# Splitting float32 weights by two GpSimd-issued DMAs and one ACT negation, in place of an ACT cast and a GpSimd subtraction

## The chip, the cores and the metric

One core of one Trainium2 chip runs the whole program in one launch. The metric is the device time of that launch in microseconds. The kernel before takes 3497.29 us (median of 3 runs, 3495.54 to 3500.16).

## The reference, cut to what matters

The model has ten parts in a row, each of them working on the same residual of 512 tokens by 1024 features in float32: twice a mixer (attention beside a gated delta net, m0 and m1) and a feed-forward layer (f0, f1), then an even mixer (ev), cross-attention with a memory (xa0), a feed-forward layer (g0), an odd mixer (od), cross-attention (xa1) and a feed-forward layer (g1). Nearly all of the arithmetic is products of activations with weights, as in the feed-forward layers of the first block:

```python
h = rmsnorm(x, norm_ffn_g[l])
u = centred_depthwise_conv(h @ w_up[l], ffn_conv_w[l])      # 1024 -> 2 * 2816
u_gate, u_val = jnp.split(u, 2, axis=-1)
x = x + ((jax.nn.silu(u_gate) * u_val) @ w_down[l])         # 2816 -> 1024
```

The products must have float32 accuracy. The kernel gets it from three products of a faster format, float32r: with w = hi + lo and a = hi' + lo', it sums hi·hi', hi·lo' and lo·hi'.

## The kernel before, in words

Activations are held feature-major, as eight chunks of 128 features by 512 tokens, each as its two float32r parts (`act`, or `mid` behind the gate of a feed-forward layer). A **group** of weights is 128 output columns times eight chunks of 128 input rows. Its product (`proj`, lines 480 to 491) is 24 matmuls into one PSUM bank: for each chunk hi with the first part of the activation (L487), hi with the second (L490), lo with the first (L491).

The weights come through `wload` (L464). One DMA on SP's queue (`fetch`, L461) brings 256 columns, 1 MB, into `wraw`, which has two buffers. Each half group, 128 columns by four chunks, is then split: ACT rounds it to float32r (`whi`, L474), GpSimd subtracts that from the raw weights (`wlo`, L475, which is recorded as L383). `whi` and `wlo` have four buffers of half a group each, so two groups are split ahead, and `wraw` holds up to four groups more.

A feed-forward layer works in 11 **pairs** (`up_pair`): it loads two groups of the gate (A and B) and two of the value (C and D), and TensorE needs them in the order A, C and B mixed, D. The results go through DVE, ACT and (in g0 and g1, `up2`) one GpSimd product `cv<-cv,rB` into `mid`. After five, nine and eleven pairs `down` adds to the residual (`out_proj`).

The instructions are put into order, engine by engine, by a scheduler that models time while the program is built; each engine then works in that order and waits for semaphores. SP's queue carries, besides the weights, all scratch transfers of the mixers.

Of the kernel before, what the change touches and what calls it, by code (L numbers as in the profile page):

```python
# [11 lines left out]
F32 = mybir.dt.float32  # L12
F32R = mybir.dt.float32r
# [48 lines left out]
def _vec_layout(inputs=None):  # L62
    """All per-feature vectors as columns of one [128, n] array; fills VEC with the places."""
# [19 lines left out]
        # (dir, pair) columns, the head of the pair by partition half  # L83
# [26 lines left out]
def _const_layout():  # L110
    """Constants of the shapes alone, [128, n] float32."""
# [94 lines left out]
def host_arrays(inputs):  # L206
# [15 lines left out]
    # z, and the rows of its product's projection: heads 0 2, 1 3, 4 6, 5 7 side by side  # L222
# [4 lines left out]
    A["win"] = _pack_cols(np.concatenate([kd, qd, vd, qa, ka, va, z, gate], axis=-1), 8, 256)  # L227
# [3 lines left out]
    A["wout"] = _pack_cols(g("w_out"), 8, 256)  # L231
    A["wup"] = _pack_cols(g("w_up"), 8, 256)
    for nm, key in (("wdn", "w_down"), ("fdn", "ffn_w_out_2")):
        w = g(key)
        A[nm] = np.concatenate([_pack_cols(w[:, :1024], 8, 256), _pack_cols(w[:, 1024:2048], 8, 256)], axis=1)
        A[nm + "c"] = _pack_cols(w[:, 2048:], 6, 256)
# [3 lines left out]
    A["evin"] = _pack_cols(np.concatenate(ev, axis=2).reshape(1, D, 4096), 8, 256)  # L240
    A["evout"] = _pack_cols(np.concatenate([eo[:, 1 - i, h] for i, h in EV_HEADS], axis=1), 8, 256)
    # by head: q, k, v columns side by side
    od = g("od_w_in_2").reshape(1, D, 3, 8, P).transpose(0, 1, 3, 2, 4).reshape(1, D, 3072)
    A["odin"] = _pack_cols(od, 8, 256)
    A["odout"] = _pack_cols(g("od_w_out_2"), 8, 256)
    A["xaq"] = _pack_cols(g("xa_w_q_2"), 8, 256)
    A["xakv"] = _pack_cols(g("xa_w_kv_2"), 8, 256)
    A["xao"] = _pack_cols(g("xa_w_o_2"), 8, 256)
    A["fup"] = _pack_cols(g("ffn_w_in_2"), 8, 256)
# [10 lines left out]
# ---------------------------------------------------------------- the program  # L260
class Norm:
    """RMS norm of the feature-major residual: chunks x*g split in two float32r parts; the
    reciprocal root of each token, on all partitions, is applied where products leave PSUM."""
# [8 lines left out]
    def chunk(self, m):  # L272
# [12 lines left out]
        # the sums of the last chunk apart, the others' are done by then  # L285
# [20 lines left out]
class Prog:  # L306
    def __init__(self, ctx, tc, A, out, first):
# [5 lines left out]
        self.wr = pool("wr", 2)  # L313
# [13 lines left out]
        # the first weights amid the residual  # L327
        self.first = []
        for m in range(8):
            nc.sync.dma_start(out=self.x[m], in_=A["x"][m])  # L330
            if m == 1:
                self.first = [self.fetch(s, 8, n) for s, n in first]
# [7 lines left out]
    def banks(self, *bufs):  # L340
        """The PSUM banks besides those of the projections, in up to three rings."""
# [11 lines left out]
    def phase(self, name):  # L353
        """The pool of a layer part: temporaries by role."""
# [3 lines left out]
    def gs(self, name, bufs=2, shape=(P, S), dt=F32):  # L358
        """A temporary of a role: its buffers go round in program order."""
# [40 lines left out]
    def issue_behind(self, ins, before):  # L400
        """Issue order on an engine, no wait."""
# [56 lines left out]
    # ---- weights  # L458
    def fetch(self, src, kc, cg):
        raw = self.wr.tile([P, kc, cg], F32, name="wraw", tag="wraw")  # L460
        self.nc.sync.dma_start(out=raw, in_=src.rearrange("p (k c) -> p k c", k=kc))  # L461
        return raw
# [1319 lines left out]
```

## Time and profile before

| | |
|---|---|
| time, median of 3 runs | 3497.29 us |
| span of the profiled execution | 3496.1 us |
| TensorE busy | 3232.1 us, 92% |
| VectorE (DVE) busy | 2028.2 us, 58% |
| ScalarE (ACT) busy | 1483.6 us, 42% |
| GpSimd (POOL) busy | 1806.7 us, 52% |
| DMA moved | 342.51 MB, mean 98 GB/s |

The profile gives no time of its own for the profiled execution beside its span of 3496.1 us, first to last instruction; that is 1.2 us under the median of the runs. PE is TensorE's matmuls and PEld its weight loads, which lie beside each other. A busy time says how long an engine had work in hand; a wait is the idle time before an instruction, put down to what ended it. Matmuls overlap in the pipeline, so the distance between their starts, not their duration, is what one costs.

The ten parts can be told apart by the copy `rB` (L303) that ends each norm. By it m0 runs from 0 to 552 us, f0 to 917, m1 to 1437, f1 to 1803, ev to about 2080, xa0 to 2302, g0 to 2669, od to about 2920, xa1 to 3141 and g1 to 3496.

### The profile page before, as it was taken

Reading aid. Unit: us, or ns where it says so; the run is one execution under the profiler, and the core shown is the slowest. Engines: PE = TensorE matmul, PEld = TensorE weight load, DVE = VectorE, ACT = ScalarE, POOL = GpSimd, SP = SyncE. Lnnn points to the kernel's source line nnn. Section 1 sums busy time; section 2 is a strip of 40 time slices with the busy share of each in tenths; the row PEclk is TensorE's granted clock in tenths of the full one; section 3 lists DMA queues with packets and bytes.
Section 4 is the critical chain, followed back from the end, with each engine's and each line's share of the span. In section 5 each row is a group of like instructions: output and inputs, shape, how many; then the busy total and the mean of one; then the engine's idle time right before and its main releaser. Section 6 shows DMA issues by size and latency. Waiting matters only on the chain. (4 is left out here: it accounts for less than half of the span.)

```text
span 3496.1 us, 46894 instructions
## 1 busy us (share of the span) xinstructions
PE 3232.1 (92%) x17342; PEld 2661.3 (76%) x17342; DVE 2028.2 (58%) x3571; ACT 1483.6 (42%) x2766; POOL 1806.7 (52%) x1493
## 2 busy tenths in 40 slices
PE   8878899999978889999999888999997799899999
PEld 6666778888766677888878777888885687878887
DVE  8988556463698855555466676552323586663222
ACT  4536434343553553434353335443433355544332
POOL 4653365444565335554456556465554235556554
PEclk9999999999999999999999999999998899999999
DMA  4532532222353244222222113222223312222222
GB/s 142 161 88 61 132 122 86 100 94 94 122 159 102 72 113 128 87 97 97 94 101 86 59 62 109 73 97 97 97 91 91 84 61 103 91 90 89 95 98 93
DMA packets 135844, 342.51 MB, mean 98 GB/s; under 512 B 43039, under 2 KB 80287, under 8 KB 106944
## 3 DMA queue, kind: packets, MB, share of 16 engines
q1 hardware_dynamic: 135328, 338.75, 30.5%
q8 instruction: 138, 2.26, 0.3%
q14 instruction: 90, 0.74, 0.1%
q10 hardware_dynamic: 288, 0.76, 0.1%
HBM read 309.53 MB, written 29.95 MB: 97 GB/s over the span
## 5 line engine op out<-in xcount | busy, mean ns | idle before, releaser
L383 POOL TENSOR_TENSOR wlo<-wraw,whi 128x512 fp32r<-128x512 f32 (+2 forms) x1044 | 1370.2, 1316 | 1449.5 <-ACT whi L474 1402.0
L474 ACT CAST whi<-wraw 128x512 fp32r<-128x512 f32 (+2 forms) x1044 | 631.4, 608 | 1134.3 <-PE psb L490 838.4
L487 PE MATMUL psb<-act,whi 128*128 128x512 f32 x1888 | 760.6, 403 | 60.3 <-DVE x L383 19.8
L491 PE MATMUL psb<-act,wlo 128*128 128x512 f32 x1888 | 752.7, 399 | 3.5 <-POOL wlo L383 3.4
L490 PE MATMUL psb<-act,whi 128*128 128x512 f32 x1888 | 755.0, 400 | 0.6 <-DVE act L277 0.6
L487 PEld LDWEIGHTS psb<-act,whi 128*128 128x128 f32 x1888 | 364.5, 193 | 140.8 <-issue 43.0
L491 PEld LDWEIGHTS psb<-act,wlo 128*128 128x128 f32 x1888 | 363.4, 192 | 81.6 <-POOL wlo L383 5.8
L490 PEld LDWEIGHTS psb<-act,whi 128*128 128x128 f32 x1888 | 364.3, 193 | 74.2 <-DVE act L277 1.9
L383 DVE TENSOR_TENSOR x<-psb,x 128x512 f32<-128x512 f32 x168 | 115.2, 689 | 378.1 <-PE psb L491 377.5
L487 PE MATMUL ps<-act,whi 128*128 128x512 f32 (+1 forms) x720 | 281.6, 391 | 3.4 <-ACT rB L303 3.4
L491 PE MATMUL ps<-act,wlo 128*128 128x512 f32 (+1 forms) x720 | 281.0, 390 | 0.0
L490 PE MATMUL ps<-act,whi 128*128 128x512 f32 (+1 forms) x720 | 281.0, 390 | 0.0
L487 PE MATMUL psb<-mid,whi 128*128 128x512 f32 x704 | 277.0, 394 | 1.0 <-DVE x L383 1.0
L491 PE MATMUL psb<-mid,wlo 128*128 128x512 f32 x704 | 276.2, 392 | 0.0
L490 PE MATMUL psb<-mid,whi 128*128 128x512 f32 x704 | 274.1, 389 | 0.0
L487 PEld LDWEIGHTS ps<-act,whi 128*128 128x128 f32 (+1 forms) x720 | 134.1, 186 | 33.8 <-ACT rB L303 4.6
L491 PEld LDWEIGHTS ps<-act,wlo 128*128 128x128 f32 (+1 forms) x720 | 134.1, 186 | 29.8 <-issue 0.8
L490 PEld LDWEIGHTS ps<-act,whi 128*128 128x128 f32 (+1 forms) x720 | 134.2, 186 | 29.3 <-issue 0.5
L491 PEld LDWEIGHTS psb<-mid,wlo 128*128 128x128 f32 x704 | 132.3, 188 | 30.3
L487 PEld LDWEIGHTS psb<-mid,whi 128*128 128x128 f32 x704 | 132.6, 188 | 29.4 <-DVE x L383 1.5
L490 PEld LDWEIGHTS psb<-mid,whi 128*128 128x128 f32 x704 | 132.3, 188 | 29.1
L383 DVE TENSOR_TENSOR cv<-ps,cv 128x512 f32<-128x512 f32 (+1 forms) x60 | 41.5, 692 | 175.8 <-PE ps L491 106.1
(437 smaller groups left out, 5712.8 us busy)
## 6 DMA issues: line engine op xcount, KB each, us to landing
wraw<-in_wup SPq DMA_DIRECT2D x44, 1024.0 KB, 4.8
wraw<-in_fup SPq DMA_DIRECT2D x44, 1024.0 KB, 4.8
wraw<-in_win SPq DMA_DIRECT2D x38, 1024.0 KB, 5.0
wraw<-in_wdn SPq DMA_DIRECT2D x16, 1024.0 KB, 4.8
wraw<-in_evin SPq DMA_DIRECT2D x16, 1024.0 KB, 4.8
wraw<-in_xakv SPq DMA_DIRECT2D x16, 1024.0 KB, 4.8
wraw<-in_fdn SPq DMA_DIRECT2D x16, 1024.0 KB, 4.9
wraw<-in_odin SPq DMA_DIRECT2D x12, 1024.0 KB, 4.8
```

Of the source, the lines that this page charges most:

```text
L383: getattr(self.nc, eng).tensor_tensor(out, a, b, op)
L474: nc.scalar.copy(hi, part)
L487: mm = nc.tensor.matmul(ps, hi[:, i], acts[k][:, 0, :n], start=k == 0, stop=False)
L490: nc.tensor.matmul(ps, hi[:, i], acts[k][:, 1, :n], start=False, stop=False)
L491: nc.tensor.matmul(ps, lo[:, i], acts[k][:, 0, :n], start=False, stop=k == kc - 1)
```

## The change

`fetch`, its pool `wraw` and the prefetch of the first weights go. `wload` now asks `parts` for each group: a DMA that GpSimd issues brings 128 columns (512 KB) from DRAM straight into `whi`, with a cast to float32r; ACT writes the negative of `whi` into `wlo`; a second DMA that GpSimd issues reads the same weights again and adds them to `wlo` in place. `whi` and `wlo` now have four buffers of a whole group each, which is the room that `wraw` gave up. In the host's layout the columns of a group now lie side by side, and `mem` of the cross-attention, which lay in `wraw`, has tiles of its own.

```diff
-    def wload(self, src, kc, cg, rows=False):
-        raw = self.first.pop(0) if self.first else self.fetch(src, kc, cg)
-        step, width = (2, cg) if rows else (4, min(P, cg))
-        def piece(k, o):
-            part = raw[:, k:min(k + step, kc), o:o + width]
-            hi, lo = (self.whl.tile(list(part.shape), F32R, name=n, tag=n) for n in ("whi", "wlo"))
-            nc.scalar.copy(hi, part)
-            self.tt(lo, part, hi.bitcast(F32), ALU.subtract, "gpsimd")
-            return k, hi, lo
+    def parts(self, src, kc, cg):
+        hi, lo = (self.whl.tile([P, 1024], F32R, name=n, tag=n)[:, :kc * cg] for n in ("whi", "wlo"))
+        nc.gpsimd.dma_start(out=hi, in_=src)
+        nc.scalar.activation(lo, hi.bitcast(F32), AF.Copy, scale=-1.0)
+        nc.gpsimd.dma_start(out=lo, in_=src, accum_op=ALU.add)
+        return [t.rearrange("p (k c) -> p k c", k=kc) for t in (hi, lo)]
+    def wload(self, src, kc, cg=256, k0=0, n=None):
+        return [[(0, *self.parts(src[:, (o * kc + k0) * w:(o * kc + k0 + n) * w], n, w))] for o in range(cg // w)]
```

The change moves instructions on every engine. On POOL, in the pairs of g0, this stood before (each `wlo` row one half group, two halves in turn to a group; `cv` is the gate's value, `rB` the norm's root):

```order
L383 TENSOR_TENSOR wlo_20874<-wraw_20863,whi_20873 128x512
L383 TENSOR_TENSOR cv_20827<-cv_20827,rB_20201 128x512
L383 TENSOR_TENSOR wlo_20878<-wraw_20863,whi_20877 128x512
L383 TENSOR_TENSOR wlo_20884<-wraw_20881,whi_20883 128x512
L383 TENSOR_TENSOR wlo_20888<-wraw_20881,whi_20887 128x512
L383 TENSOR_TENSOR wlo_20892<-wraw_20881,whi_20891 128x512
```

and now, one pair of g0 (A is 19332, B 19337, C 19342, D 19347, and 19476 is A of the next pair):

```order
L470 DMA wlo_19333<-in_fup 128x1024
L387 TENSOR_TENSOR cv_19234<-cv_19234,rB_19022 128x512
L468 DMA whi_19337<-in_fup 128x1024
L468 DMA whi_19342<-in_fup 128x1024
L470 DMA wlo_19338<-in_fup 128x1024
L387 TENSOR_TENSOR cv_19296<-cv_19296,rB_19022 128x512
L470 DMA wlo_19343<-in_fup 128x1024
L468 DMA whi_19347<-in_fup 128x1024
L468 DMA whi_19476<-in_fup 128x1024
L470 DMA wlo_19348<-in_fup 128x1024
L470 DMA wlo_19477<-in_fup 128x1024
```

The subtractions are gone, and in their place stand two DMA issues for each group: the high parts of B and C, then their low parts, then the high parts of D and the next A, then their low parts.

On PE, at the end of A in a pair of g0, this stood before (A's last half is 20869, B's first half 20873, C's first half 20883):

```order
L491 MATMUL psb_20899<-act_20168,wlo_20870 128x512
L487 MATMUL psb_20961<-act_19992,whi_20873 128x512
L490 MATMUL psb_20961<-act_19992,whi_20873 128x512
L491 MATMUL psb_20961<-act_19992,wlo_20874 128x512
L487 MATMUL psb_20961<-act_20011,whi_20873 128x512
L490 MATMUL psb_20961<-act_20011,whi_20873 128x512
L491 MATMUL psb_20961<-act_20011,wlo_20874 128x512
```

and now (A is 19476, B 19481, C 19486):

```order
L496 MATMUL psb_19496<-act_18989,wlo_19477 128x512
L492 MATMUL ps1_19528<-act_18813,whi_19486 128x512
L495 MATMUL ps1_19528<-act_18813,whi_19486 128x512
L492 MATMUL psb_19558<-act_18813,whi_19481 128x512
L495 MATMUL psb_19558<-act_18813,whi_19481 128x512
L496 MATMUL psb_19558<-act_18813,wlo_19482 128x512
L492 MATMUL psb_19558<-act_18832,whi_19481 128x512
L496 MATMUL ps1_19528<-act_18813,wlo_19487 128x512
```

Before, B's first half followed A alone. Now two matmuls of C and four of B come first and then the one that needs C's low part: within seven matmuls of A's end all four tiles of B and C are in use.

## Rows read from the trace of the kernel before

**Rows 1.** Busy time by stage: window, its length, engines (instructions), granted clock, DMA share, GB/s.
```profile
0.00:552.00 552.00, 470.93 (x3202) 377.67 (x3203) 410.12 (x687) 260.44 (x510) 283.98 (x257) 0.96 0.41 116
552.00:917.00 365.00, 364.00 (x1607) 299.56 (x1605) 193.46 (x227) 150.83 (x247) 186.60 (x145) 1.00 0.29 103
917.00:1437.00 520.00, 452.02 (x3129) 365.94 (x3128) 389.85 (x649) 244.46 (x484) 266.49 (x232) 0.96 0.39 110
1437.00:1803.00 366.00, 364.44 (x1607) 299.93 (x1605) 196.55 (x240) 150.36 (x245) 186.40 (x144) 1.00 0.28 99
2302.00:2669.00 367.00, 366.15 (x1614) 302.20 (x1615) 112.72 (x159) 141.45 (x226) 208.46 (x166) 1.00 0.28 96
3141.00:3496.00 355.00, 350.64 (x1540) 288.83 (x1540) 99.01 (x135) 123.97 (x197) 189.47 (x151) 1.00 0.27 95
```

**Rows 2.** Waits of PE over the span: who waited for whom, us in total, times, longest.
```profile
PE ps L1568 <- DVE pr L1570: 44.0, 1, 44.0
PE psb L487 <- DVE x L383: 21.8, 15, 3.8
...
PE psb L487 <- DVE N L383: 11.8, 2, 6.1
PE ps L796 <- DVE cv L513: 11.6, 2, 6.0
...
PE ps L412 <- DVE kq L725: 8.1, 2, 4.0
PE psb L487 <- DVE pad L383: 7.9, 4, 2.9
...
PE psb L491 <- POOL wlo L383: 4.2, 5, 1.1
```

**Rows 3.** Timeline of PE in g1: start, us, instruction; 56 matmuls from first to last.
```profile
3159.63 0.39 PE L490 MATMUL psb<-act,whi 128*128 128x512 f32 x1
...
3172.32 0.39 PE L487 MATMUL ps<-act,whi 128*128 128x512 f32 x1
```

**Rows 4.** Costliest groups, forms apart: count | busy us, mean ns | idle before, releasers.
```profile
L383 POOL TENSOR_TENSOR wlo<-wraw,whi 128x512 fp32r<-128x512 f32 x992 | 1330.5, 1344 | 1420.3 <-ACT whi L474 1372.8 <-PE psb L491 33.9 <-PE psb L490 4.7
...
L474 ACT CAST whi<-wraw 128x512 fp32r<-128x512 f32 x992 | 611.1, 619 | 1082.5 <-PE psb L490 791.9 <-PE ps L490 143.4 <-POOL wlo L383 52.4
...
L474 ACT CAST whi<-wraw 128x256 fp32r<-128x256 f32 x48 | 19.4, 405 | 50.2 <-PE psb L490 45.4 <-PE ps L490 3.0 <-PE psb L491 1.3
```

**Rows 5.** DMA issues: out<-in, queue, count, KB each, median us from issue to landing.
```profile
wraw<-in_wup SPq DMA_DIRECT2D x44, 1024.0 KB, 4.8
wraw<-in_fup SPq DMA_DIRECT2D x44, 1024.0 KB, 4.8
...
wraw<-in_xao SPq DMA_DIRECT2D x16, 512.0 KB, 3.7
...
wraw<-in_odout SPq DMA_DIRECT2D x8, 512.0 KB, 3.8
...
N<-scrT SPq DMA_DIRECT2D x2, 1024.0 KB, 13.3
```

**Rows 6.** Timeline in a pair of g1, the queue of SP: one weight issue.
```profile
3209.96 0.33 SPq L461 DMA_DIRECT2D wraw<-in_fup  x1
```

**Rows 7.** The same stretch, POOL: one gate product.
```profile
3207.39 1.29 POOL L383 TENSOR_TENSOR cv<-cv,rB 128x512 f32<-128x512 f32 x1
```

**Rows 8.** DVE's instructions of three lines: count, ns min/median/max, first and last start.
```profile
L589 DVE SCALAR_TENSOR_TENSOR cv<-pad,vect,cv x88: 739/753/1849, 555.3 to 1759.1; 128x512 f32<-128x512 f32 x88
L695 DVE SCALAR_TENSOR_TENSOR kq<-pad,vect,kq x64: 730/752/1839, 31.6 to 974.5; 128x512 f32<-128x512 f32 x64
L695 DVE SCALAR_TENSOR_TENSOR cv<-pad,vect,cv x32: 735/752/1771, 90.6 to 1046.8; 128x512 f32<-128x512 f32 x32
```

**Rows 9.** Costliest groups, forms apart, DVE: the same lines' mean.
```profile
L589 DVE SCALAR_TENSOR_TENSOR cv<-pad,vect,cv 128x512 f32<-128x512 f32 x88 | 107.6, 1225 | 2.3
...
L695 DVE SCALAR_TENSOR_TENSOR kq<-pad,vect,kq 128x512 f32<-128x512 f32 x64 | 65.5, 1037 | 5.7 <-ACT kq L693 5.1
```

**Rows 10.** Windows around od's long wait (columns as in rows 1).
```profile
2690.00:2734.00 44.00, 0.22 (x2) 0.00 (x0) 0.23 (x1) 2.00 (x3) 0.00 (x0) 0.50 0.53 84
2734.00:2737.00 3.00, 2.83 (x9) 2.55 (x10) 2.77 (x9) 1.10 (x4) 0.00 (x0) 0.50 0.09 32
2737.00:2740.00 3.00, 3.00 (x9) 2.36 (x8) 2.72 (x15) 0.71 (x2) 0.00 (x0) 0.52 0.00 0
```

More of the change, by code (lines that the diff above doesn't have):

```diff
@@ L51, in _pack_cols, with _pack_tiles @@
     return np.ascontiguousarray(a).reshape(L, g, P, kc * cg)
+def _pack_tiles(w, kc):
+    a = _pack_cols(w, kc, 256)
+    L, g = a.shape[:2]
+    return np.ascontiguousarray(a.reshape(L, g, P, kc, 2, P).transpose(0, 1, 2, 4, 3, 5)).reshape(L, g, P, kc * 256)
 def _cols(v):
@@ L226, in host_arrays @@
     ka = ka[..., PERM_A]
-    A["win"] = _pack_cols(np.concatenate([kd, qd, vd, qa, ka, va, z, gate], axis=-1), 8, 256)
+    A["win"] = _pack_tiles(np.concatenate([kd, qd, vd, qa, ka, va, z, gate], axis=-1), 8)
     A["wbd"] = _pack_cols(bd, 8, 32)
@@ L230, in host_arrays @@
     A["wod"] = _pack_cols(by_head(g("w_o_dn").transpose(0, 2, 1)).transpose(0, 2, 1), 4, 128)
-    A["wout"] = _pack_cols(g("w_out"), 8, 256)
-    A["wup"] = _pack_cols(g("w_up"), 8, 256)
+    A["wout"] = _pack_tiles(g("w_out"), 8)
+    A["wup"] = _pack_tiles(g("w_up"), 8)
     for nm, key in (("wdn", "w_down"), ("fdn", "ffn_w_out_2")):
         w = g(key)
-        A[nm] = np.concatenate([_pack_cols(w[:, :1024], 8, 256), _pack_cols(w[:, 1024:2048], 8, 256)], axis=1)
-        A[nm + "c"] = _pack_cols(w[:, 2048:], 6, 256)
+        A[nm] = np.concatenate([_pack_tiles(w[:, :1024], 8), _pack_tiles(w[:, 1024:2048], 8)], axis=1)
+        A[nm + "c"] = _pack_tiles(w[:, 2048:], 6)
     ev, eo = g("ev_w_in_2").reshape(1, D, 8, 4, P), g("ev_w_out_2").reshape(1, 2, 4, P, D)
     ev = [ev[:, :, 5]] + [ev[:, :, (slice(0, 4), [4, 6, 7])[i == 0], h] for i, h in EV_HEADS]
-    A["evin"] = _pack_cols(np.concatenate(ev, axis=2).reshape(1, D, 4096), 8, 256)
-    A["evout"] = _pack_cols(np.concatenate([eo[:, 1 - i, h] for i, h in EV_HEADS], axis=1), 8, 256)
+    A["evin"] = _pack_tiles(np.concatenate(ev, axis=2).reshape(1, D, 4096), 8)
+    A["evout"] = _pack_tiles(np.concatenate([eo[:, 1 - i, h] for i, h in EV_HEADS], axis=1), 8)
     od = g("od_w_in_2").reshape(1, D, 3, 8, P).transpose(0, 1, 3, 2, 4).reshape(1, D, 3072)
[L244 to L249, printed above, removed]
+    A["odin"] = _pack_tiles(od, 8)
+    A["odout"] = _pack_tiles(g("od_w_out_2"), 8)
+    A["xaq"] = _pack_tiles(g("xa_w_q_2"), 8)
+    w = g("xa_w_kv_2")
+    A["xakv"] = np.concatenate([_pack_tiles(w[..., :1024], 8), _pack_cols(w[..., 1024:], 8, 256)], axis=1)
+    A["xao"] = _pack_tiles(g("xa_w_o_2"), 8)
+    A["fup"] = _pack_tiles(g("ffn_w_in_2"), 8)
     return A
@@ L306, with __init__ @@
 class Prog:
-    def __init__(self, ctx, tc, A, out, first):
+    def __init__(self, ctx, tc, A, out):
         self.ctx, self.tc, self.nc, self.A, self.out = ctx, tc, tc.nc, A, out
@@ L326, in __init__ @@
         nc.scalar.dma_start(out=self.cst, in_=A["cst"])
-        self.first = []
         for m in range(8):
             nc.sync.dma_start(out=self.x[m], in_=A["x"][m])
-            if m == 1:
-                self.first = [self.fetch(s, 8, n) for s, n in first]
         self.ident = self.c("ident")
@@ L456, in spread, with wrows @@
         return ps
[L459 to L462, printed above, removed]
-    def wload(self, src, kc, cg, rows=False):
-        nc = self.nc
-        raw = self.first.pop(0) if self.first else self.fetch(src, kc, cg)
-        step, width = (2, cg) if rows else (4, min(P, cg))
-        def piece(k, o):
-            part = raw[:, k:min(k + step, kc), o:o + width]
-            hi, lo = (self.whl.tile(list(part.shape), F32R, name=n, tag=n) for n in ("whi", "wlo"))
-            nc.scalar.copy(hi, part)
-            self.tt(lo, part, hi.bitcast(F32), ALU.subtract, "gpsimd")
-            return k, hi, lo
-        return [[piece(k, o) for k in range(0, kc, step)] for o in range(0, cg, width)]
+    def parts(self, src, kc, cg):
+        nc = self.nc
+        hi, lo = (self.whl.tile([P, 1024], F32R, name=n, tag=n)[:, :kc * cg] for n in ("whi", "wlo"))
[4 more added lines that the diff above has]
+    def wload(self, src, kc, cg=256, k0=0, n=None):
+        n = n or kc
+        w = min(P, cg)
+        return [[(0, *self.parts(src[:, (o * kc + k0) * w:(o * kc + k0 + n) * w], n, w))] for o in range(cg // w)]
+    def wrows(self, src, kc):
+        n = kc // 2
+        return [(k, *self.parts(src[:, k * 256:(k + n) * 256], n, 256)) for k in (0, n)]
     def proj(self, ps, w, acts, n=S, behind=None):
@@ L533, in out_proj @@
         for g in range(4):
-            ws = self.wload(wsrc[g][:, k0 * 256:(k0 + kc) * 256], kc, 256)
+            ws = self.wload(wsrc[g], wsrc[g].shape[-1] // 256, k0=k0, n=kc)
             for j in range(2):
@@ L1633, in queries @@
             return qs, roots(sqs, 1.0, 256 * EPS, S, nm)
-        mem = self.wr.tile([P, 8, M], F32, name="wraw", tag="wraw")
-        nc.sync.dma_start(out=mem, in_=self.A["mem"].rearrange("p (k m) -> p k m", k=8))
+        mem = [xp.tile([P, 4, M], F32, name=f"mem{i}", tag=f"y{6 + i}") for i in range(2)]
+        for i in range(2):
+            nc.sync.dma_start(out=mem[i], in_=self.A["mem"].rearrange("p (i k m) -> p i k m", i=2, k=4)[:, i])
         q0 = queries(0)
@@ L1643, in _cross @@
             g = self.vec(f"xm{l}", k)
-            hi = nc.scalar.activation(a[:, 0], mem[:, k], AF.Copy, scale=g)
-            lo = nc.vector.scalar_tensor_tensor(a[:, 1], mem[:, k], g, a[:, 0].bitcast(F32), ALU.mult, ALU.subtract)
+            hi = nc.scalar.activation(a[:, 0], mem[k // 4][:, k % 4], AF.Copy, scale=g)
+            lo = nc.vector.scalar_tensor_tensor(a[:, 1], mem[k // 4][:, k % 4], g, a[:, 0].bitcast(F32), ALU.mult, ALU.subtract)
             if k == 0:
@@ L1651, in _cross @@
             sq = xp.tile([P, 4, M], F32, name="msq", tag="pT", bufs=3)
-            nc.scalar.activation(sq, mem[:, 4 * h:4 * h + 4], AF.Square)
+            nc.scalar.activation(sq, mem[h], AF.Square)
             nc.gpsimd.tensor_tensor(sq[:, 0:2], sq[:, 0:2], sq[:, 2:4], ALU.add)
@@ L1678, in _cross @@
                 self.split(kn[-1], x)
-            ws = self.wload(wkv[4 + h], 8, 256, rows=True)
+            ws = self.wrows(wkv[4 + h], 8)
             vt = [gs("vt", 4, (P, 2, M), F32R) for _ in range(2)]
@@ L1684, in _cross @@
                 o = pv[t][:, :M]
-                for k, hi, lo in ws[0]:
-                    for i in range(2):
+                for k, hi, lo in ws:
+                    for i in range(4):
                         nc.tensor.matmul(o, ma[k + i][:, 0, tok], hi[:, i], start=k + i == 0, stop=False)
@@ L1731, in _cross @@
                     nc.tensor.matmul(po, vt[k][:, 0, c], pT[1][:, k], start=False, stop=k == 1)
[L1732 removed]
+                y = xp.tile([P, 2, S], F32R, name=f"y{2 * h + i}", tag=f"y{2 * h + i}")
                 self.split(y, po)
@@ L1746, in body @@
     with ExitStack() as ctx:
-        k = Prog(ctx, tc, A, out, [(A["wbd"][0, 0], 32), (A["win"][0, 0], 256)] if phases[0] == "m0" else [])
+        k = Prog(ctx, tc, A, out)
         norms = [Norm(k, _NORM[p], i == 0) for i, p in enumerate(phases)] + [None]
```

2 lines of the change are left out of this document (removed).

## The prediction

> **What bounds the kernel now.** I read the busy times by stage first [rows 1]: in the four feed-forward layers TensorE is busy in all but 1 to 4 us of each, 1453 us together (365 + 366 + 367 + 355), at the full granted clock. In m0 and m1 it is busy for 471 of 552 and 452 of 520 us, so 149 us stand idle there. Next the waits of PE [rows 2]: apart from one of 44.0 us in od, they are small and mostly on DVE; for the weights' low part it waits 4.2 us in the whole span. So the subtraction that goes, 992 times 1344 ns on POOL [rows 4], is 1330 us of an engine that holds TensorE up for 4.2 us. The reader is to see in that row that POOL itself sat idle 1420 us before these subtractions, and waited for ACT, which waited in turn for PE to free a buffer. The weights run ahead of their use; TensorE's rate is the bound. The timeline gives that rate [rows 3]: (3172.32 - 3159.63) / 56 = 0.2266 us a matmul, so a group of 24 takes 5.44 us and a pair of four groups 21.8 us.
>
> It follows that removing POOL's work can win little, and that the question is whether the new way still delivers a group each 5.44 us, early enough.
>
> **What a group costs in the new way.** It is a chain: issue of the high part, landing, negation on ACT, issue of the low part, landing.
> - *Plain transfer.* 512 KB take 3.7 to 3.8 us from issue to landing, 1 MB 4.8 [rows 5], so each further 512 KB in flight adds about 1.0.
> - *High part.* They are issued two at a time, so 4.8 with the neighbour beside it. No row shows a DMA issued by POOL or one with a cast. Below, such an issue holds its engine 0.33 us as on SP [rows 6]; above, 1.29 as POOL's own 128x512 instruction [rows 7]; I take 0.8, near the middle, which is 0.5 more than what the 4.8 already hold. High part: 5.3.
> - *Negation.* ACT takes 619 ns for 512 columns and 405 for 256 [rows 4]: 214 ns for 256 more, so 1.05 us for 1024. That is 0.19 less than the two casts, a gain that ends no wait of PE.
> - *Low part.* No row shows an accumulating DMA. It must read the weights and its own destination, so I count it as twice the bytes: 4.8, with a neighbour of the same kind beside it 2.0 more, and 0.5 for the issue: 7.3. Below stands the plain 3.8; above, 13.3 us, the slowest 1 MB transfer of this kernel [rows 5], a scattered one. I take 7.3, since these rows are long and contiguous like the weights'.
>
> **What it meets in a feed-forward layer.** POOL works in order. In the new order the high part of B stands ahead of that of C, and B's waits until PE is through with the last pair's B. From there PE has D and the next A to do, 10.88 us, and six matmuls, 1.36, and then needs C's low part: 12.24 us. The chain to it: C's issue behind B's 0.8, high part 5.3, negation 1.05, low part 7.3: 14.45 in f0 and f1. In g0 and g1 POOL has `cv<-cv,rB` between the two low parts: B's low part is issued at 5.3 + 1.05 = 6.35, 0.8 for it and 1.29 for the product [rows 7] make 8.44, and with 7.3 the landing is at 15.74. Late by 2.2 and 3.5 us, once a pair. The 44 loads of 1 MB for each up projection [rows 5], two to a pair, make 22 pairs each: 22 x 2.2 + 22 x 3.5 = 125 us. The down projections use their groups in the order of loading, three groups ahead, 16.3 us against 14.5 to 15.7, and cost nothing; without that cover they would cost as the pairs do.
>
> **The other parts of the model.** Of 992 half groups, 496 groups, the feed-forward layers use 4 x 66 = 264 (44 up, 22 down), so 232 are left for the remaining 2043 us (3496 - 1453), 8.8 us each instead of 5.44. The price by group in the layers was 125 / 176 = 0.71 us. More time between groups covers more, but here POOL's own work and ACT's stand in the same queues, and a DMA issue that waits for a buffer or for ACT now holds up the mixers' products behind it, for which DVE waits. I take half, 0.36 x 232 = 83 us; the bounds are nothing and the full 165.
>
> **The gain.** DVE's conv products with two SBUF inputs have a median of 753 ns and reach 1849 [rows 8]; their mean is 1225 and 1037 [rows 9]. The subtraction on POOL, which reads the same memory, is the likely cause. In f0 and f1 this lies beside PE. In the mixers 96 of them (64 and 32) could lose 0.285 us each, 27 us of DVE; the waits of PE on DVE that it could shorten sum to 61 us (21.8 + 11.8 + 11.6 + 8.1 + 7.9) [rows 2]. I take 20, between 0 and 61. The Trainium skill, "SBUF — State Buffer", on the shared GpSimd and vector port, states that a vector instruction with two SBUF inputs contends with a GpSimd instruction that reads SBUF; the spread of that one form agrees. By it alone the kernel would be faster by these 20 us.
>
> The freed SP queue wins nothing that I can see: the 44.0 us of od are the landing of od's own bias table, not of weights.
>
> **Sum.** 3496.1 + 125 + 83 - 20 = 3684 us, and 1.2 us from the span to the median of the runs: 3685.
>
> **The rivals.**
> *The weights stay ahead, and it is faster.* If the POOL-issued transfers land as SP's do, the chain is 0.33 + 3.8 + 1.05 + 3.8 = 9.0 us (10.3 in g0 and g1, with the 1.29): below 12.24. Then PE never waits and only the gain is left, 3497 - 20 = 3477, down to 3436 with all 61. For it: the same bytes in the same rows. Against it: a second read of each weight, and a destination that is read as well. It decides at a high and a low part that together take less than 12.24 - 0.8 - 1.05 = 10.4 us (9.1 in g0 and g1 with the product between). A rule that speaks for it: the Trainium skill, "DMA: Bandwidth & Descriptors", on the anatomy of a GpSimd-issued DMA, gives 2.0 us plus the bytes at 436 GB/s; by it 512 KB take an estimated 3.2 us, so the chain would fit and the feed-forward layers would not change. SP's 3.8 here is above that.
>
> *The transfers become the bound.* In the feed-forward layers the weights alone keep the DMA engines 27 to 29% busy [rows 1]. The high part takes that once, the low part twice if it counts as read, read: 0.28 x 3 = 0.84, still below 1. If the accumulation takes three or four times a plain transfer, it is 1.12 or 1.40, and these layers take 1453 x 0.12 = 174 or 1453 x 0.40 = 581 us more; with 13.3 for the low part, 6.8 for the high part (2 MB in flight, 4.8 + 2.0) and 1.05 + 0.8, the chain is 21.95, late by 9.7 (11.0), 455 us in the layers. The other parts then add by the rule above 0.5 x 455 / 176 x 232 = 300. So 3850 to 4250. Against it: nothing in the rows says that an accumulation is so slow; nothing says that it isn't.
>
> *The clock falls too.* In od's 44 us wait the granted clock went to 0.50, the lower level (1.2 GHz), and stayed there for some 6 us after it [rows 10]. If the waits of 2 to 4 us did that, a group would take 24 x 0.2266 more, 5.4 us a pair, 239 us in all: 3925. The waits of that length in rows 2 lie in stages at 0.96, so I give it little, as part of the case above.
>
> **Chances.** My forecast, slower by 1 to 9% (3530 to 3810): 0.52. The transfers or the clock as a bound, above 3810: 0.26. Faster: 0.15. The rest, 0.07, lies between, of which 0.05 within 0.2% (about what a measurement of this kernel can tell from no change) and 0.02 just above. So faster 0.15, same 0.05, slower 0.80. The range runs from 3465, which takes in most of the faster case, to 4200, which takes in most of the slow one; the forecast's own is 3530 to 3810.
>
> **What would show it.** The low part's landing time, 7.3, is the step that matters: below 5 I am wrong, and above 9 the second rival is right. Waits of PE for `wlo` at L496 should be some 2 to 4 us, once a pair, at the change from A to C and B, and none in the down projections. POOL's issues should take 0.8 each. The up projections' DMA share should be near 0.8. DVE's means at L594 and L700, where these conv products now stand, should fall toward 0.75 us. A trace in which PE waits in the mixers for DVE or POOL more than for weights would show the half that I took there for what it is, a choice.

## The result, and the profile after

The changed kernel takes 4127.63 us (median of 4 runs, 4123.77 to 4149.05) against 3497.8 us on the same chip: ratio 1.181, 95% interval 1.178 to 1.184. It is 630 us slower, where the forecast said 187 (3685): the side was right, the size under a third of it. The profiled execution has a span of 4127.2 us.

By the windows between the norms' copies `rB`, now at L312 (columns as in [rows 1]; here f0, f1, g0, g1):

```profile
604.00:1079.00 475.00, 401.58 (x1596) 315.74 (x1596) 149.12 (x224) 135.21 (x177) 106.44 (x145) 0.92 0.67 150
...
1639.00:2114.00 475.00, 397.34 (x1596) 313.17 (x1596) 150.68 (x233) 136.41 (x177) 104.73 (x143) 0.94 0.66 148
...
2696.00:3145.00 449.00, 397.82 (x1621) 315.66 (x1622) 103.79 (x159) 124.57 (x157) 134.29 (x166) 0.94 0.70 155
...
3698.00:4127.00 429.00, 375.68 (x1536) 299.12 (x1536) 94.18 (x134) 108.03 (x132) 119.22 (x149) 0.95 0.69 156
```

In [rows 1] TensorE was busy in all but 1 to 4 us of f0, f1, g0 and g1, at a clock of 1.00. Now 51 to 78 us of each are idle, and the clock is 0.92 to 0.95. From one `rB` to the next, the four layers take 1827.8 us together against 1446.3 before (+381), and the rest of the program 2299.4 against 2049.8 (+250). The 1446.3 go by the starts of the copies themselves; the windows of [rows 1] sum to 1453, mostly because f0's window ends at 917 and the copy stands at 913.5.

The landings (columns as in [rows 5]):

```profile
whi<-in_wup POOLq DMA_DIRECT2D x88, 512.0 KB, 7.3
...
whi<-in_fup POOLq DMA_DIRECT2D x88, 512.0 KB, 6.9
wlo<-in_fup POOLq DMA_DIRECT2D x88, 512.0 KB, 6.4
```

The high part lands after 6.9 to 7.3 us (5.3 forecast), the low part after 6.4 (7.3 forecast). Their sum, 13.3 to 13.7, is about the 12.6 that I had reckoned. The waits over the span, all engines, largest first (columns as in [rows 2]):

```profile
POOL wlo L470 <- ACT wlo L469: 2029.7, 455, 10.3
...
ACT wlo L469 <- DMA whi<-in_fup: 329.4, 61, 10.5
ACT wlo L469 <- DMA whi<-in_wup: 310.7, 61, 10.6
POOL whi L468 <- PE psb L496: 267.6, 109, 30.1
```

The first row is the one to see. POOL stands idle for 2029.7 us, half the span, in front of low-part issues, until ACT has negated the high part; ACT in turn waits for that high part to land. Against it, POOL waits only 267.6 us for TensorE to free a buffer (339 with the smaller rows of that kind). In [rows 4] it was the other way round: the weights waited for TensorE.

A stretch of g0 in the timeline of POOL (start, us, instruction, and in brackets the idle time before it and what ended it):

```profile
2760.89 0.89 POOL L470 DMA_DIRECT2D wlo<-in_fup  x1 [5.60 <-ACT wlo L469]
2762.55 0.88 POOL L470 DMA_DIRECT2D wlo<-in_fup  x1 [0.77 <-ACT wlo L469]
...
2764.86 0.59 POOL L468 DMA_DIRECT2D whi<-in_fup  x1
2766.12 0.54 POOL L468 DMA_DIRECT2D whi<-in_fup  x1 [0.67 <-PE psb L496]
2773.57 0.89 POOL L470 DMA_DIRECT2D wlo<-in_fup  x1 [6.91 <-ACT wlo L469]
2776.51 0.88 POOL L470 DMA_DIRECT2D wlo<-in_fup  x1 [2.05 <-ACT cv L608]
2777.09 1.63 POOL L387 TENSOR_TENSOR cv<-cv,rB 128x512 f32<-128x512 f32 x1
2779.07 0.59 POOL L468 DMA_DIRECT2D whi<-in_fup  x1 [0.35 <-PE ps L496]
...
2790.84 0.90 POOL L468 DMA_DIRECT2D whi<-in_fup  x1
```

The two negations of the same batch on ACT, between the issues at 2766.12 and 2776.51:

```profile
2772.22 1.06 ACT L469 ACTIVATE wlo<-whi 128x1024 fp32r<-128x1024 f32 x1 [5.93 <-DMA whi<-in_fup]
...
2773.89 1.04 ACT L469 ACTIVATE wlo<-whi 128x1024 fp32r<-128x1024 f32 x1
```

And PE, where the low part of C is needed:

```profile
2770.94 0.79 PE L496 MATMUL ps<-act,wlo 128*128 128x512 f32 x1 [2.93 <-DMA wlo<-in_fup]
2771.53 0.63 PE L492 MATMUL ps<-act,whi 128*128 128x512 f32 x1
2771.96 0.63 PE L495 MATMUL ps<-act,whi 128*128 128x512 f32 x1
...
2776.65 0.48 PE L492 MATMUL ps<-act,whi 128*128 128x512 f32 x1
```

Two high parts go out, then POOL stands for 6.91 us, then two low parts go out, and only behind them the next two high parts, from 2779.07 on; the batch after those begins at 2790.84. A batch of two groups takes 14.2 and 11.8 us here; over the layers it is 1827.8 / 132 = 13.85. TensorE needs one each 10.88. The low part that it lacks at 2770.94 is one of the batch before, issued at 2762.55 behind such a stand of 5.60 us. So it waits 2.93 us, and then works on at 0.427 us a matmul (2771.96 - 2771.53) in place of 0.2266 [rows 3] until 2776.65. The granted clock of that stretch (columns as in [rows 10], which showed the same after od's wait):

```profile
2764.00:2768.00 4.00, 3.66 (x15) 2.39 (x14) 1.98 (x3) 0.62 (x1) 2.00 (x3) 1.00 1.01 193
2768.00:2771.00 3.00, 0.07 (x2) 0.06 (x1) 0.00 (x0) 0.00 (x0) 0.00 (x0) 0.84 1.02 315
2771.00:2774.00 3.00, 3.00 (x7) 2.42 (x8) 0.00 (x0) 1.78 (x3) 0.43 (x1) 0.50 0.23 83
...
2777.00:2780.00 3.00, 3.00 (x15) 2.45 (x14) 0.69 (x1) 0.17 (x1) 2.31 (x3) 1.00 1.06 182
```

An idle stretch of 3 us, and behind it TensorE works at the lower level (0.50, 1.2 GHz) for nearly 6 us.

The 381 us of the four layers, from the starts of their matmuls: distances over 0.6 us, less one matmul, come to 80.2 + 82.8 + 55.6 + 52.5 = 271 (f0, f1, g0, g1), and the matmuls at the lower clock to 32.1 + 28.2 + 25.5 + 22.0 = 108 more. By the idle time before them, 266 us in all, the waits for C's low part are 87 (41 waits), for a gate group's low part (A, B) 43, for the low parts of the down projections 86, and for high parts 10; the remaining 40 lie at the borders of the layers and in a few single waits.

### The profile page after: what moved, and what is told of

It reads as the page before. It is cut to its first block, busy times and chain, and to the rows that moved or that the text cites. A ratio compares the mean times of both kernels' runs of the same rounds, so it can differ in the third digit from the quotient of the medians.

```text
span 4127.2 us, 45943 instructions
## 1 busy us (share of the span) xinstructions
PE 3429.5 (83%) x17342; PEld 2750.5 (67%) x17342; DVE 1703.0 (41%) x3571; ACT 1391.0 (34%) x2296; POOL 1239.6 (30%) x1597
## 2 busy tenths in 40 slices
DMA packets 257659, 609.10 MB, mean 148 GB/s; under 512 B 56575, under 2 KB 98175, under 8 KB 256928
## 4 chain that ended last, share of the span: by engine, by line
issue 22%; DMA 17%; PE 9%; POOL 7%; ACT 4%; DVE 1%; POOLq 0%; ACTq 0%; SPq 0%; DVEq 0%
DMA whi<-in_fup 4%; POOL wlo L470 3%; POOL whi L468 3%; ACT wlo L469 3%; DMA whi<-in_fdn 3%; DMA whi<-in_xakv 2%; PE psb L496 2%; PE psb L492 2%; PE psb L495 2%; DMA whi<-in_wup 2%; DMA wlo<-in_fup 1%; DMA whi<-in_odin 1%; POOL cv L387 1%; DMA whi<-in_evin 1%; PE ps L496 1%
## 5 line engine op out<-in xcount | busy, mean ns | idle before, releaser
L469 ACT ACTIVATE wlo<-whi 128x1024 fp32r<-128x1024 f32 (+3 forms) x574 | 550.5, 960 | 1949.8 <-DMA whi<-in_fup 329.4
L496 PE MATMUL ps<-act,wlo 128*128 128x512 f32 (+1 forms) x720 | 309.5, 430 | 87.3 <-DMA wlo<-in_wup 46.6
L496 PE MATMUL psb<-mid,wlo 128*128 128x512 f32 x704 | 292.1, 415 | 86.1 <-DMA wlo<-in_wdn 38.2
L492 PE MATMUL ps<-act,whi 128*128 128x512 f32 (+1 forms) x720 | 303.8, 422 | 29.7 <-ACT rB L312 19.2
L495 PE MATMUL ps<-act,whi 128*128 128x512 f32 (+1 forms) x720 | 300.5, 417 | 0.0
L492 PE MATMUL psb<-mid,whi 128*128 128x512 f32 x704 | 287.3, 409 | 11.8 <-ACT mid L501 11.8
L495 PE MATMUL psb<-mid,whi 128*128 128x512 f32 x704 | 286.1, 407 | 0.4 <-DVE mid L503 0.4
L496 PEld LDWEIGHTS ps<-act,wlo 128*128 128x128 f32 (+1 forms) x720 | 147.9, 205 | 140.0 <-DMA wlo<-in_wup 55.7
L470 POOL DMA_DIRECT2D wlo<-in_wup x88 | 76.4, 869 | 479.6 <-ACT wlo L469 479.6
L492 PEld LDWEIGHTS ps<-act,whi 128*128 128x128 f32 (+1 forms) x720 | 148.3, 206 | 65.2 <-ACT rB L312 20.4
L470 POOL DMA_DIRECT2D wlo<-in_fup x88 | 77.8, 885 | 361.0 <-ACT wlo L469 345.2
L495 PEld LDWEIGHTS ps<-act,whi 128*128 128x128 f32 (+1 forms) x720 | 147.3, 205 | 34.9
L492 PEld LDWEIGHTS psb<-mid,whi 128*128 128x128 f32 x704 | 138.8, 198 | 44.5 <-ACT mid L501 13.7
```

The lines of the kernel that those rows point to most:

```text
L469: nc.scalar.activation(lo, hi.bitcast(F32), AF.Copy, scale=-1.0)
L470: nc.gpsimd.dma_start(out=lo, in_=src, accum_op=ALU.add)
L492: mm = nc.tensor.matmul(ps, hi[:, i], acts[k][:, 0, :n], start=k == 0, stop=False)
L495: nc.tensor.matmul(ps, hi[:, i], acts[k][:, 1, :n], start=False, stop=False)
L496: nc.tensor.matmul(ps, lo[:, i], acts[k][:, 0, :n], start=False, stop=k == kc - 1)
```

## The experiments

Theory P: POOL's queue in its order is the cause. The low part's issue waits there for a landing and a negation, and the next high part, though its buffer is mostly free, stands behind it. Rivals: the lead of four buffers is too short (L), the transfers are the bound (T), ACT's queue is held by waiting negations (A). Times are medians of 4 runs (10 for e3), ratios stand against the kernel before on the same chip; "layers" is f0 + f1 + g0 + g1 between copies of `rB`, "rest" the span without them, both of the one profiled execution. The scheduler orders the program anew for each edit, so parts that an edit doesn't touch move too, by up to 62 us in the rest.

| run | time, us | ratio (95%) | layers | rest |
|---|---|---|---|---|
| before | 3497.8 | 1 | 1446.3 | 2049.8 |
| after | 4127.63 | 1.181 (1.178 to 1.184) | 1827.8 | 2299.4 |
| e1_acbd | 4083.19 | 1.168 (1.163 to 1.173) | 1788.5 | 2318.9 |
| e2_ffn8 | 4080.40 | 1.166 (1.163 to 1.169) | 1796.2 | 2271.6 |
| e3_cut | 3495.27 | 0.998 (0.997 to 1.000) | 1453.1 | 2043.7 |
| e4_plainlo | 3605.47 | 1.030 (1.026 to 1.033) | 1533.7 | 2069.4 |
| e5_actwait | 3572.01 | 1.021 (1.019 to 1.023) | 1486.4 | 2084.9 |
| e6_poolwait | 4312.68 | 1.233 (1.230 to 1.235) | 2041.6 | 2273.2 |
| e7_poolneg | 4423.76 | 1.265 (1.262 to 1.268) | 2024.7 | 2413.1 |
| e8_ahead3 | 3792.76 | 1.084 (1.081 to 1.086) | 1538.5 | 2237.4 |
| e9_ahead1 | 3825.38 | 1.092 (1.089 to 1.095) | 1552.0 | 2270.6 |
| e10_ahead1_acbd | 3771.99 | 1.076 (1.073 to 1.080) | 1480.5 | 2291.0 |
| e11_allahead | 3625.19 | 1.035 (1.033 to 1.038) | 1478.7 | 2142.2 |

**e1_acbd: a pair is loaded in the order A, C, B, D.**

```diff
-                wg = self.wload(wup[mp], 8, 256)
-                wv = self.wload(wup[11 + mp], 8, 256)
...
+                for o in range(2):
+                    wg.append(one(wup[mp], o))
+                    wv.append(one(wup[11 + mp], o))
```

> Only the order of loading in a pair of the feed-forward up projections changes: A, C, B, D, as TensorE uses them, in place of A, B, C, D. Theory L (lead): the loss is a chain of issue, landing, negation, issue, landing that is longer than the time from a buffer's release to its next use, and in the pairs the order of loading makes that time short (12.2 us for C). Then the waits of PE on lo in the up projections go, the down projections' stay, and the time falls by about 210 us to some 3915 (3870 to 3970). Theory T (throughput): POOL's queue and the DMA engines deliver a group only every 6.5 us or so, whatever the order: within 30 us of 4128.

The time falls by 44 us of 630: more than the 30 that theory T allowed, far from L's 210, so neither expectation holds as it stands. The place where C's low part is needed, on which my forecast rested, is not what decides. The 39 us of the layers are a rough figure, because the profiled execution, 4109.15 us, is the longest of the four, and its granted clock in the layers is 0.82 to 0.84 (f0; columns as in [rows 1]):

```profile
613.70:1083.80 470.10, 421.38 (x1596) 315.25 (x1596) 148.55 (x224) 135.55 (x177) 106.89 (x146) 0.82 0.67 152
```

Most of its matmuls stand 0.24 to 0.27 us apart in place of 0.2266, and yet it is only 26 us above the median: TensorE's own rate does not bound these layers any more.

**e2_ffn8: eight buffers of each part in the layers.**

`deep(4)` opens a pool of four more buffers, which the groups take by fours in turn with the old ones (in part):

```diff
-        with self.phase("ffn") as fp, self.banks(2, 2):
+        with self.phase("ffn") as fp, self.banks(2, 2), self.deep(4):
```

> The feed-forward layers get eight buffers of a whole group each instead of four (four of them in a pool of their own); nothing else changes. Theory L: the release of a buffer then lies four groups (21.8 us) further ahead, the waits in all four layers go and with them the low clock: minus 340 to 380 us, 3750 to 3790. Theory T: the first few groups of each layer come earlier, then the rate binds again: 4050 to 4128, and the DMA share in the layers stays near 0.7.

The layers gain 32 us: the lead alone, L, does not explain the loss. With twice the buffers POOL still stands before its low parts (the waits; the line is now L479):

```profile
POOL wlo L479 <- ACT wlo L478: 1944.6, 457, 10.6
```

In POOL's timeline in f1 it stands there for 7.45 and 8.88 us, and three groups go out between 1701.05 and 1722.35, 7.1 us for each:

```profile
1701.05 0.86 POOL L479 DMA_DIRECT2D wlo<-in_wup  x1 [8.13 <-ACT wlo L478]
...
1710.46 0.88 POOL L479 DMA_DIRECT2D wlo<-in_wup  x1 [7.45 <-ACT wlo L478]
1712.03 0.88 POOL L479 DMA_DIRECT2D wlo<-in_wup  x1 [0.68 <-ACT wlo L478]
...
1722.35 0.85 POOL L479 DMA_DIRECT2D wlo<-in_wdn  x1 [8.88 <-ACT wlo L478]
```

TensorE needs one each 5.44. Its own waits are put down to other things here (95.1 us in the span to DVE's `pad`, 66.0 to ACT's `mid`); the rate of the layers is nearly the same with four buffers and with eight (6.92 and 6.80 us a group). One of these waits, in f0, from the timelines of ACT, DVE and PE:

```profile
719.42 1.06 ACT L478 ACTIVATE wlo<-whi 128x1024 fp32r<-128x1024 f32 x1 [4.77 <-DMA whi<-in_wdn]
...
721.12 0.75 DVE L602 SCALAR_TENSOR_TENSOR cv<-pad,vect,cv 128x512 f32<-128x512 f32 x1 [6.54 <-ACT cv L601]
...
725.41 0.80 PE L501 MATMUL psb<-mid,whi 128*128 128x512 f32 x1 [9.79 <-DVE pad L394]
```

ACT stands before a negation until its high part lands, DVE waits for the ACT instruction behind that negation, and TensorE waits for DVE. Followed back in this way, 212 of TensorE's 235 us of waits in the layers lead to ACT waiting for a high part, and only 11 are waits for a low part. So the buffers did take away the waits for weights; but the high parts still leave POOL too late, and the loss now comes through ACT's queue. So A has a part in e2, and e5 had to tell what it costs by itself.

**e3_cut: the low part no longer depends on the high part, with every transfer, buffer and instruction count kept.**

```diff
-        nc.scalar.activation(lo, hi.bitcast(F32), AF.Copy, scale=-1.0)
+        nc.scalar.activation(lo, self.vect[:, 0:1].broadcast_to((P, kc * cg)), AF.Copy, scale=-1.0)
```

> ACT fills lo from one column of constants instead of from hi's negative, so the sums are not those of the reference; the same bytes move by the same issues and ACT still writes 1024 columns a group, but the low part no longer waits for the high part's landing. Theory L: the chain loses about 7 us everywhere, in the mixers too: 3520 to 3620. Theory T: the traffic is the same, so 4000 to 4128.

All of the loss is gone, in the layers and in the rest. The same 609.10 MB are moved, in 15% less time, and in f0 the DMA engines are busy for 0.92 of the time while TensorE misses 0.5 of 363 us:

```profile
561.00:924.00 363.00, 362.48 (x1596) 298.39 (x1596) 152.58 (x224) 135.61 (x176) 104.81 (x144) 1.00 0.92 196
```

And the waits over its span:

```profile
POOL whi L468 <- PE psb L496: 1116.8, 348, 22.3
...
POOL wlo L470 <- ACT wlo L469: 363.5, 399, 24.2
```

T falls: the transfers can be delivered at the needed rate. POOL now waits mostly for TensorE, as the weights did in [rows 4]. What costs is the dependence alone; where it costs, e4 to e6 had to tell.

**e4_plainlo: the second transfer does not accumulate.** It casts to float32r, as the first one does.

```diff
-        nc.gpsimd.dma_start(out=lo, in_=src, accum_op=ALU.add)
+        nc.gpsimd.dma_start(out=lo, in_=src)
```

> The second DMA copies the weights over lo instead of adding to it, so lo holds the weights and the sums are not those of the reference; issues, waits and bytes from DRAM are the same, only the read of the destination goes. Theory A: the accumulation is what makes both transfers slow (they share a queue), so the high part's landing falls from 7.0 to about 5 and the low part's from 6.4 to about 4.5, and the chain of 14.5 to 10.5 fits: 3600 to 3750. Rival: a transfer issued by POOL, or one with a cast, takes 6 to 7 us by itself: the high part stays above 6 and the time above 3950.

```profile
whi<-in_fup POOLq DMA_DIRECT2D x88, 512.0 KB, 5.2
wlo<-in_fup POOLq DMA_DIRECT2D x88, 512.0 KB, 4.3
```

Both landings become shorter, the low part by 2.1 us and the high part, which the edit doesn't touch, by 1.7. With a chain of that length POOL's order is still the same, and the kernel is 104 us above the one before on its chip (3501.25) in place of 630. So the accumulation makes the chain long, and the order makes its length count. The Trainium skill, "Collectives: The Full Stack", in its section on the bandwidth ceiling, says of collectives that the one that reduces is slower than the one that copies because the add needs two source reads. For the DMA of this kernel, which is no collective, 6.4 against 4.3 us agrees in kind, at 1.5 times.

**e5_actwait and e6_poolwait: the wait for the high part on one engine alone.** In both, DVE fills the low part from a constant column; then a small read of the high part (8 columns) stands once on ACT, and once on POOL ahead of the low part's issue.

```diff
-        nc.scalar.activation(lo, hi.bitcast(F32), AF.Copy, scale=-1.0)
+        nc.vector.tensor_copy(lo, self.vect[:, 0:1].broadcast_to((P, kc * cg)))
+        seen = self.nrm.tile([P, 8], F32, name="seen", tag="seen", bufs=4)
+        nc.scalar.activation(seen, hi[:, :8].bitcast(F32), AF.Copy, scale=-1.0)
```

and in e6, in place of the last of these lines:

```diff
+        look = nc.gpsimd.tensor_copy(seen, hi[:, :8].bitcast(F32))
+        acc = nc.gpsimd.dma_start(out=lo, in_=src, accum_op=ALU.add)
+        self.issue_behind(acc, look)
```

> DVE fills lo from one column of constants, so the sums are not those of the reference; ACT only reads eight columns of hi, and so still waits in its queue for each high part's landing, while POOL's low part does not wait for it. Theory P: it is POOL's queue that lost the time, since the low part's issue waits there for landing and negation and the next high part's issue stands behind it; ACT's waiting costs little. Then within 60 us of 3500. Rival A: ACT's queue lost it, since conv, gelu and split stand behind a negation that waits for a landing, and DVE and PE behind them: 3700 or more.

> As the run before, but now POOL reads eight columns of hi in front of each low part's issue, and ACT does not touch the weights (the sums are not those of the reference). POOL's queue holds high part, wait, low part, one group at a time. Theory P: each group costs POOL the high part's landing (5.5 us with nothing beside it) and two issues, some 7 us against the 5.44 that TensorE needs, so the feed-forward layers take 264 x 1.6 = 420 us more, the rest about as much again: 3900 to 4300. Rival A: with ACT free it is 3500 to 3600.

ACT waits for 338.3 + 325.1 us on the up projections' high parts in e5, no less than with the change (310.7 + 329.4), and the kernel is 2.1% slower than before, 73 us, DVE's 574 fills included. That is 12 us above what P allowed and far below A's 3700: while POOL's queue moves on, ACT's waiting is at most a small part. With the wait on POOL, and no arithmetic on the path, the kernel is slower than the changed one (13 us above the range that P had named, which had put the high part's landing at 5.5 us; it is 6.6 to 6.9 in the up projections here). Here POOL takes one group at a time, and from one high part to the next there pass 7.1 and 8.0 us, the landing and two issues; the product `cv` of the second lies inside its landing (columns as above):

```profile
2857.58 0.87 POOL L468 DMA_DIRECT2D whi<-in_fup  x1
2863.48 0.70 POOL L471 COPY seen<-whi 128x8 f32<-128x8 f32 x1 [5.03 <-DMA whi<-in_fup]
2864.13 0.86 POOL L472 DMA_DIRECT2D wlo<-in_fup  x1
2864.69 0.86 POOL L468 DMA_DIRECT2D whi<-in_fup  x1
2865.26 1.60 POOL L387 TENSOR_TENSOR cv<-cv,rB 128x512 f32<-128x512 f32 x1
...
2872.73 0.85 POOL L468 DMA_DIRECT2D whi<-in_fup  x1
```

The layers need 264 groups; 2041.6 / 264 = 7.73 us for each. P stands.

**e7_poolneg: the negation on POOL too, so that POOL waits for no other engine between the two issues.**

```diff
-        nc.scalar.activation(lo, hi.bitcast(F32), AF.Copy, scale=-1.0)
+        nc.gpsimd.tensor_scalar(lo, hi.bitcast(F32), -1.0, None, ALU.mult)
```

> The negation moves from ACT to POOL and the sums are the reference's again. ACT then never waits for a landing; POOL's chain is longer by the negation (about 1 to 2.5 us a group) and shorter by one change of engine. Theory P: slower than 4128, by 50 to 300 us. Rival A: faster than 4050, since ACT's queue is free.

The costliest group of POOL (columns as in [rows 4]):

```profile
L469 POOL TENSOR_SCALAR wlo<-whi 128x1024 fp32r<-128x1024 f32 x436 | 1240.3, 2846 | 825.1 <-issue 210.0 <-DMA whi<-in_wup 170.1 <-DMA whi<-in_fup 107.8
```

POOL takes 2846 ns for what ACT does in 1057 and still waits for the landing. Worse, as P has it.

**e8_ahead3: high parts three groups ahead of low parts on POOL, eight buffers, in the layers only.** In part:

```diff
+        while self.todo and len(self.begun) < self.look + 1:
+            self.begun.append(self.start(*self.todo.pop(0)))
+        return self.finish(*self.begun.pop(0))
...
+            self.issue_behind(neg, self.last_hi)
+            self.issue_behind(acc, self.last_hi)
```

> In the feed-forward layers alone, eight buffers, and on POOL's queue the high part of a group stands three groups ahead of its low part (the negation likewise waits for that order), so that no issue waits for a landing that was only just begun; the sums are the reference's. Theory P: the layers lose their 381 us, the mixers keep their 249: 3740 to 3800, against 4080 with eight buffers in the old order. Rival T, the DMA engines or POOL's time for issues: above 3950. Rival A: ACT still waits, above 3900.

The buffers alone had won 32 us (e2); with the order it is 289 of the layers' 381. In these rows of g0 POOL sends a group each 5.5 us, and waits for TensorE only:

```profile
2624.18 0.56 POOL L477 DMA_DIRECT2D whi<-in_fup  x1 [4.00 <-PE psb L518]
2624.72 0.90 POOL L482 DMA_DIRECT2D wlo<-in_fup  x1
2629.67 0.55 POOL L477 DMA_DIRECT2D whi<-in_fup  x1 [4.05 <-PE psb L518]
```

**e9_ahead1 and e10_ahead1_acbd: the order without the buffers.** One group ahead, four buffers as in the change; e10 also loads A, C, B, D (the edit of e1). Against e8, in part:

```diff
-        self.fw, self.np, self.todo, self.begun, self.look = None, 0, None, [], 3
+        self.fw, self.np, self.todo, self.begun, self.look = None, 0, None, [], 1
-        with self.phase("ffn") as fp, self.banks(2, 2), self.deep(4):
+        with self.phase("ffn") as fp, self.banks(2, 2):
```

> The feed-forward layers (f0, f1, g0, g1) keep their four buffers of a group; only POOL's order changes there: the high part of the next group is issued one group ahead of each low part (three ahead and eight buffers in the run before, 1538.5 us for the four layers; 1827.8 with the change as it stands, 1446.3 before it). Sums are the reference's. If POOL's order is the cause by itself, a low part no longer finds a wait for its own high part, and the layers come to 1540 to 1680, the whole to 3800 to 3950. If four buffers are too few without the depth, because the high part of the next group waits on POOL for TensorE to free one and the low part behind it waits too, the layers stay at 1750 or above and the whole at 4050 or above.

> As the run with one group ahead and four buffers, but a pair's groups are also loaded in the order in which TensorE needs them, A, C, B, D. If POOL's order is the cause, and the load order matters only once POOL's order is right, the layers come to 1500 to 1600 us and the whole to 3760 to 3880, below the run with A, B, C, D by 30 to 100. If buffers are the limit, both runs are at 1750 or above in the layers.

e9 lies where P had it: one group ahead alone gives back 276 of the layers' 381 us. e10 is better than I expected: 1480.5, so the two orders together give back 347, with the same transfers, tiles, negations and instructions as the change. The load order, worth 44 us of time in e1, is worth 53 here, 72 in the layers. The edit of e8 to e11 puts each negation, too, behind the next high part's issue, so ACT's order moves with POOL's; e5 and e6 tell the two apart. ACT still waits 578 us for high parts in the layers of e10, and TensorE loses hardly anything by it.

**e11_allahead: the same for every weight of the program.** The program is built twice, and the first build only notes the order of the weights. Against e10, in part:

```diff
-            self.todo = ups(0, 5) + downs(0) + ups(5, 9) + downs(1) + ups(9, 11) + downs(2)
...
+    todo = None
+    for _ in range(2):
...
+            todo = body(tc, A, out, todo=todo)
```

> The same order as in the run with one group ahead, four buffers and A, C, B, D, now for every weight of the program: in the mixers, ev, od, xa0 and xa1 too the high part of the next group stands on POOL ahead of each low part, across the borders of the parts of the model as well. Sums are the reference's. Before, these six parts and the start take 2049.8 us, with the change 2299.4, in the run above 2291.0. If their loss has the same cause as that of the feed-forward layers, they come back to 2060 to 2130, and the whole to 3530 to 3620. If in the mixers another thing costs (POOL's products held up behind issues that wait for a buffer, ACT's negations in ACT's queue, the accumulation's traffic beside the scratch transfers), they stay at 2200 or above and the whole at 3670 or above.

The rest of the program comes back from 2299.4 to 2142.2, a little above the 2130 I had given, and the whole to 3625.19, 5 us above. So the mixers' and projections' loss has the same cause for 157 of its 250 us. In all, POOL's order, with the pairs' load order, is 502 of the 630 us, and 127 are left. In the rest, TensorE's waits sum to 253 us before, 425 with the change and 330 in e11. Those for DVE and ACT went from 230 to 320 and are back at 209; those for low parts went from almost nothing to 87 and are still 96. These lie in the following rows above all (waits of PE over the span; the low matmul is L525, in the value part of xa0 and xa1 L1726):

```profile
PE psb L1726 <- DMA wlo<-in_xakv: 23.8, 10, 4.2
...
PE psb L525 <- DMA wlo<-in_win: 19.7, 7, 4.9
```

The 92 that are left in the rest are of the size of these waits; I took the 127 no further apart. No version here beats the kernel before: e3, which has everything except the dependence, shows how far a better order could get, and that is 0.0 to 0.3% below it.

## Why the prediction was wrong in size

*What bounds the kernel.* Right: TensorE's rate was the bound, POOL's time was worth little. POOL's busy time fell by 567 us (1806.7 to 1239.6), and where nothing else stood in the way (e3) that was worth 6 us.

*The chain of a group.* Nearly right in sum: 0.8 + 5.3 + 1.05 + 7.3 = 14.45 was forecast; 7.0, 1.06 and 6.4 were measured, the issues 0.5 to 0.9 of POOL's time. The high part was priced at 5.3, beside a second high part; in e4, without an accumulation, it takes 5.2, so the 1.7 us more come from the accumulations that the change's order puts beside it.

*Late once a pair, at C.* Of right size by itself: 87 us in 41 waits, 125 forecast. **The step that failed is what it was embedded in.** I counted that chain once against a lead of buffers (14.45 against 12.24) and took POOL to be free for the next group meanwhile. It isn't: I had written that POOL works in order, and for the mixers even that an issue that waits for ACT holds up the products behind it, but not that it holds up the next high part. The low part's issue stands there until its own high part has landed and been negated. So a batch of two costs POOL a landing, a negation, four issues and what else stands between them, 13.85 us by the layers' time, against 10.88 needed. That is a rate and not a lead: it falls on A and B (43 us) and on every later load too.

*The down projections cost nothing.* Wrong for the same reason: 86 us in 41 waits. Being three groups ahead in use doesn't help if the queue falls behind in every batch.

*The other parts, 83 us.* Measured 250. I halved a price that was too low, on the argument that more time between groups covers more; e11 shows that POOL's order holds them up as well. The 232 are whole groups by their size; many weights there come in smaller pieces, and the chain is run 310 times (574 negations less 264). The other half of my reason fits: TensorE's waits for DVE and ACT grew by 90 us there, about as much as those for low parts, 87.

*The gain, 20 us.* The mechanism was right in the main: most of DVE's conv products are back at their short form (columns as in [rows 9], now at L594 and L700):

```profile
L594 DVE SCALAR_TENSOR_TENSOR cv<-pad,vect,cv 128x512 f32<-128x512 f32 x88 | 65.9, 751 | 2.8
L700 DVE SCALAR_TENSOR_TENSOR kq<-pad,vect,kq 128x512 f32<-128x512 f32 x64 | 47.7, 752 | 12.9 <-ACT kq L698 12.1
L700 DVE SCALAR_TENSOR_TENSOR cv<-pad,vect,cv 128x512 f32<-128x512 f32 x32 | 31.2, 976 | 7.3 <-ACT cv L698 7.0
```

1225 ns became 751 and 1037 became 752; the 32 `cv` of L700 only went from 1042 to 976, and what lengthens them stays open. The gain lay beside other work: e3 has the same short products and is 0.2% below the kernel before, some 6 us.

*The rivals.* "The transfers become the bound" named 3850 to 4250, which holds the time, but for a reason that e3 refutes, so that is luck. Only its upper end follows from its terms; with the same rule for the other parts, an accumulation of three times a plain transfer gives 3786 and one of four times 4461. "The clock falls too" was right as a mechanism: 108 us of the layers' 381. I had dismissed it because waits of 2 to 4 us in [rows 2] lay in stages at 0.96; a mean over 500 us doesn't show what follows one wait of 3 us.

*What the profile was to show.* The low part at 7.3 us was to be "the step that matters"; it came at 6.4, better than forecast, and the loss was more than three times the forecast's. The DMA share of the layers was to be near 0.8; it was 0.66 to 0.70, since nothing kept the queue filled. The sign I should have asked for is POOL's own wait ahead of the low part's issue. The Trainium skill, "DMA: Bandwidth & Descriptors", in its anatomy of a GpSimd-issued DMA, says that a DMA's semaphore wait happens on the issuing sequencer before dispatch; the 2029.7 us of POOL in front of L470 agree. It was the rule to weigh, in place of that section's 2.0 us plus bytes, by which 512 KB would take an estimated 3.2 us and which every median landing of 512 KB shown here exceeds (from POOL 4.3 and more).

## What to carry to other kernels

Here a DMA that had to wait for other work held POOL's queue, and so every load behind it. For a load in two steps, count what one turn of the queue takes (landing, work between, issues) and divide by the groups that go out in one turn; here that was 6.92 us against the consumer's 5.44, twice the buffers won 32 of 381 us, and issuing the first step of the next group ahead of the second step of this one won 276 without any. Before pricing a wait once, ask whether it comes again in each turn, and add the matmuls at half clock behind it.

## What the hardware showed that I had not expected

- A DMA from POOL of 512 KB into float32r, beside one that accumulates: medians of 5.3 to 7.3 us for the cast, 6.3 to 7.9 for the accumulation, in the layers of after and e8 to e11; without an accumulation (e4) 5.2 and 4.3 in g0 and g1. Where one of each goes at a time (e8 to e11), the cast takes 5.3 to 6.0 although an accumulation is beside it. Each issue takes 0.5 to 0.9 us of POOL.
- With the DMA engines busy for 0.92 of f0 (e3) TensorE lost nothing, though two transfers of 512 KB for each group stood in their queue.
- In one wait of 2.93 us the granted clock fell to 0.50 and stayed there for some 6 us behind it: that cost 13 matmuls 0.2 us each, 2.6 us, almost as much again as the wait.
